# Expert MLP on one core: the last two results in one tile of 8 KB rows, and two weight loads cut differently

## The chip, the core and the metric

One core of a Trainium2 chip runs the kernel. The metric is device time in microseconds (us). Each number of the kernel before is from three runs, or from one further execution taken with the hardware profiler. The engines are named as in the profile: PE multiplies, PEld loads weights for it, DVE, ACT and POOL are the vector, scalar and general engines, and SP only issues transfers. SP, ACT and POOL each have a queue (SPq, ACTq, POOLq) in which instructions wait in order. All transfers are carried by the core's 16 DMA engines; the profile calls POOL's transfer queue q0, SP's q1, ACT's q10, and q8 and q14 carry instructions.

## The reference

Eight experts, each with 256 tokens (`capacity`), a hidden size of 512 and an inner size of 2048, all float32:

```
h   = maximum(x @ w1 + b1, 0)     # [8, 256, 2048]
out = h @ w2 + b2                 # [8, 256, 512]
```

The inputs `w1` and `w2` are 4 MB per expert each. The output is 512 KB per expert, 4 MB in all.

## The kernel before, in words

The names: `E` is 8 experts, `T` 256 tokens, `H` 512, `M` 2048, `P` 128 partitions, `nTB` = 2 token blocks, `nKC` = 4 slices of H, `nJ` = 16 slices of M. All weights are read by POOL's transfers, which cast float32 to float16 on the way: 2 MB land in SBUF for each 4 MB read. `w1_pool` and `w2_pool` hold three experts each.

The loop at the end of the function has E + LAG steps (`LAG` = 3). Step `s` makes the first product of expert `s` and the second product of expert `s - 3`. The first product (`first_product`) makes `hT` in 16 slices, each of four matmuls into `ph` and one ACT activation with the bias. The second product (`second_product`) starts two PSUM tiles `po0` and `po1`, one for each token block, with a one-row matmul that adds b2, and then adds 16 matmuls to each. It goes through `w2` in the same pieces in which `w2` was loaded: for a whole tile, first all 16 matmuls of `po0` and then all 16 of `po1`; for a tile in halves, 8 matmuls of `po0` and 8 of `po1` with the first half, and then the same with the second. PE's matmuls keep the order of the program (`ordered`), and so do POOL's transfers.

The order of the loads is written into a list, `ring`: at step `s` those entries are put into POOL's queue whose step has come. The loads of `w2` stand there in the order of the experts, and behind the last of them stand the two stores that `flush` makes, 2 MB for experts 0 to 3 and 1 MB for experts 4 and 5.

Results are gathered in `store`. `GROUPS` says which experts share a tile: 0 to 3 with rows of 16 KB, 4 and 5 with rows of 8 KB. In a group of n experts the token order is such that each expert fills P/n partitions with rows of n * nTB * H values. ACT's activation writes `hT` in the matching order (`split`), and DVE copies `po0` in n pieces and ACT `po1` in n pieces. Experts 6 and 7 are in no group: each has a tile of its own from `out_pool`, with rows of 4 KB, one DVE copy and one ACT copy. Expert 6 is stored in three parts, 25 rows by SP, 96 by ACT and 7 by SP (`PARTS`), and expert 7 by SP in one transfer of 128 rows, which is the last thing that the kernel starts. `HALVED` names the experts whose `w2` is loaded and used in halves: 6 and 7.

Of the kernel before, what the change touches and what calls it, by code (L numbers as in the profile page):

```python
# [10 lines left out]
def kernel(  # L11
# [9 lines left out]
    nc = tc.nc  # L21
    fp32 = mybir.dt.float32
    fp16 = mybir.dt.float16
    E, T, H = x.shape
    M = w1.shape[2]
    P = 128
    nTB = T // P
    nKC = H // P
    nJ = M // P
    B = 32  # L30
    nB = P // B
    LAG = 3

    GROUPS = {0: 4, 4: 2}
    HALVED = (E - 2, E - 1)


    PARTS = {E - 2: ((0, 25, False), (25, 121, True), (121, 128, False))}  # L40
    nXF32 = 2
    X_LOADS = {2: 2, 4: 4}

    def ordered(ins):
        return tc.keep_in_program_order(ins)
# [7 lines left out]
    group_pool = ctx.enter_context(tc.tile_pool(name="groups", bufs=1))  # L53
    out_pool = ctx.enter_context(tc.tile_pool(name="outp", bufs=2))
# [11 lines left out]
    w2_sb = [None] * E  # L66
    hT = [None] * E
    pending = {}
    results = {}
    group_of = {first + i: (first, n) for first, n in GROUPS.items() for i in range(n)}  # L70

    def load_x(first, n):

        R = n * T // P
        t = x_pool.tile([P, R, H], fp16, tag=f"x{first}", name=f"x{first}")
        ordered(nc.gpsimd.dma_start(  # L76
            out=t, in_=x[first : first + n].rearrange("e (p r) h -> (e p) r h", r=R)
        ))
        for i in range(n):
            x16[first + i] = (t, i * (P // n), R)  # L80
# [7 lines left out]
    def load_w2(e):  # L88
        src = w2[e].rearrange("(p j) h -> p j h", j=nJ)
        w2_sb[e] = w2_pool.tile([P, nJ, H], fp16, tag="w2", name="w2sb")  # L90
        half = nJ // 2 if e in HALVED else nJ
        for lo in range(0, nJ, half):
            ordered(nc.gpsimd.dma_start(out=w2_sb[e][:, lo : lo + half], in_=src[:, lo : lo + half]))  # L93

    def transposes(e):


        t, p0, R = x16[e]
        n = R // nTB
        xT[e] = xT_pool.tile([P, nKC, T], fp16, tag="xT", name="xT")  # L100
        for g in range(T // R // B):
            src = t[p0 + B * g : p0 + B * (g + 1)]
            for b in range(nB):
                block = src[:, :, b * (H // nB) : (b + 1) * (H // nB)].rearrange(
                    "p (n tb) (i kc) -> p tb kc n i", tb=nTB, kc=nKC)
                out = xT[e][b * B : (b + 1) * B].rearrange(
                    "p kc (tb g i n) -> p tb g kc n i", tb=nTB, i=B, n=n)
                if n == 1:
                    nc.vector.transpose(out=out[:, :, g, :, 0, :], in_=block[:, :, :, 0, :])  # L109
                    continue  # L110
                for tb in range(nTB):
                    nc.vector.transpose(out=out[:, tb, g], in_=block[:, tb])  # L112

    def first_product(e):
        hT[e] = hT_pool.tile([P, nJ, T], fp16, tag="hT", name="hT")
        split = group_of[e][1] if e in group_of else 1
        for j in range(nJ):
            bias_at = j * B + e * nB + nB - 1
            ph = psum_h.tile([P, T], fp32, tag="ph", name="ph")
            for kc in range(nKC):  # L120
                ordered(nc.tensor.matmul(  # L121
                    out=ph,
                    lhsT=w1_sb[e][:, kc, :].rearrange("p (q j) -> p q j", j=nJ)[:, :, j],
                    rhs=xT[e][:, kc, :],
                    start=(kc == 0),
                    stop=(kc == nKC - 1),
                ))
            nc.scalar.activation(  # L128
                out=hT[e][:, j, :].rearrange("p (tb k i) -> p tb k i", tb=nTB, k=split),
                in_=ph.rearrange("p (tb i k) -> p tb k i", tb=nTB, k=split),  # L130
                func=mybir.ActivationFunctionType.Relu,
                bias=b1T[:, bias_at : bias_at + 1],
                scale=1.0,
            )
            if j == nJ // 2 and e + 1 < E:
                transposes(e + 1)
# [3 lines left out]
        ordered(nc.gpsimd.dma_start(out=dst, in_=src))  # L140

    def store(e, po):
        if e in group_of:
            first, n = group_of[e]
            split, rows = n, P // n
            if e == first:
                results[e] = group_pool.tile(
                    [P, split * nTB, H], fp32, tag=f"out{e}", name=f"out{e}")
        else:
            first, n, split, rows = e, 1, 1, P  # L150
            results[e] = out_pool.tile([P, nTB, H], fp32, tag="out", name="out")
        out_sb = results[first]
        at = (e - first) * rows
        for k in range(split):
            part = slice(k * rows, (k + 1) * rows)
            nc.vector.tensor_copy(out=out_sb[at : at + rows, k * nTB, :], in_=po[0][part])  # L156
            nc.scalar.copy(out=out_sb[at : at + rows, k * nTB + 1, :], in_=po[1][part])  # L157
        dst = out[first : first + n].rearrange("e (p r) h -> (e p) r h", r=split * nTB)
        if e in group_of:
            if e == first + n - 1:  # L160
                pending[first] = (dst, out_sb)
            return
        for p0, p1, scalar in PARTS.get(e, ((0, P, False),)):
            (nc.scalar if scalar else nc.sync).dma_start(out=dst[p0:p1], in_=out_sb[p0:p1])

    def second_product(e):
        po = []
        for tb in range(nTB):
            t = psum_o.tile([P, H], fp32, tag=f"po{tb}", name=f"po{tb}")
            po.append(t)  # L170
            ordered(nc.tensor.matmul(  # L171
                out=t, lhsT=ones1, rhs=b2_sb[0:1, e * H : (e + 1) * H], start=True, stop=False,
            ))
        half = nJ // 2 if e in HALVED else nJ
        for lo in range(0, nJ, half):
            for tb in range(nTB):
                for j in range(lo, lo + half):
                    ordered(nc.tensor.matmul(  # L178
                        out=po[tb],
                        lhsT=hT[e][:, j, tb * P : (tb + 1) * P],  # L180
                        rhs=w2_sb[e][:, j, :],
                        start=False,
                        stop=(j == nJ - 1),
                    ))
        store(e, po)

    x32 = []
    for e in range(nXF32):
# [4 lines left out]
        out=b2_sb,  # L193
        in_=b2.rearrange("e h -> (e h)").rearrange("(o f) -> o f", o=1),
# [12 lines left out]
    for b in range(nB):  # L207
        nc.vector.transpose(  # L208
            out=b1T[b * B : (b + 1) * B, nB - 1 - b : nB - 1 - b + nJ * B],
            in_=b1_rows.rearrange("r (i j) -> r j i", j=nJ),  # L210
# [4 lines left out]
    ring = []  # L215
    for s in range(1, E + LAG - 1):
        if s < E:
            if s in X_LOADS:
                ring.append((s - 2, load_x, (s, X_LOADS[s])))
            ring.append((s - 2, load_w1, (s,)))  # L220
        if s >= LAG:
            ring.append((s - 2, load_w2, (s - LAG,)))
    ring.append((E + LAG - 3, load_w2, (E - 1,)))
    for first, n in GROUPS.items():
        ring.append((first + n + LAG, flush, (first,)))

    for s in range(E + LAG):
        while ring and ring[0][0] <= s:
            _, put, args = ring.pop(0)
            put(*args)  # L230
        if s < E:
            first_product(s)
        if s >= LAG:
            second_product(s - LAG)
# [31 lines left out]
```

## Time and profile before

| | us |
|---|---|
| median of 3 runs (lowest to highest) | 181.59 (181.48 to 181.77) |
| the profiled execution, own time | 181.45 |
| its span in the trace | 179.7 |
| PE busy in the span | 129.1 |
| DVE busy | 88.0 |
| ACT busy | 70.2 |
| last matmul ends | 173.31 |
| last store issued by SP | 173.9 |

The span begins with the first instruction and ends with the last one. Sums on the trace are made in the span's time; the profiled execution took 1.75 us more than its span, and lies 0.14 us under the median. Besides instructions the trace holds one record for each DMA packet, with its queue, size, start and duration, but without the engine that carried it. A packet here is one row of a transfer: 16 KB, 8 KB or 4 KB as it is written.

### The profile page before, as it was taken

Reading aid. Unit: us, or ns where it says so; the run is one execution under the profiler, and the core shown is the slowest. Engines: PE = TensorE matmul, PEld = TensorE weight load, DVE = VectorE, ACT = ScalarE, POOL = GpSimd, SP = SyncE. Lnnn points to the kernel's source line nnn. Section 1 sums busy time; section 2 is a strip of 40 time slices with the busy share of each in tenths; the row PEclk is TensorE's granted clock in tenths of the full one; section 3 lists DMA queues with packets and bytes.
Section 4 is the critical chain, followed back from the end, with each engine's and each line's share of the span. In section 5 each row is a group of like instructions: output and inputs, shape, how many; then the busy total and the mean of one; then the engine's idle time right before and its main releaser. Section 6 shows DMA issues by size and latency. Waiting matters only on the chain.

```text
span 179.7 us, 1958 instructions
## 1 busy us (share of the span) xinstructions
PE 129.1 (72%) x784; PEld 85.8 (48%) x784; DVE 88.0 (49%) x125; ACT 70.2 (39%) x151; POOL 13.1 (7%) x28
## 2 busy tenths in 40 slices
PE   0005099969595970899969597969497887999950
PEld 0004079969592320795369244844195332433420
DVE  0999942987000199999999998003200020301010
ACT  0000459969593022483099005950586020020010
POOL 7000002120201010001010001000200021010000
PEclk9999999999998798589999889999999996999996
DMA  5999999999999999999999999999999999999996
GB/s 216 251 226 199 233 212 197 233 224 193 228 230 192 221 233 215 197 230 230 204 208 230 219 193 233 226 193 222 230 215 197 233 206 204 223 212 215 335 420 250
DMA packets 3829, 40.56 MB, mean 226 GB/s; under 512 B 461, under 2 KB 477, under 8 KB 1133
## 3 DMA queue, kind: packets, MB, share of 16 engines
q0 software_dynamic: 3232, 38.35, 96.6%
q1 hardware_dynamic: 476, 1.70, 2.4%
q10 hardware_dynamic: 112, 0.39, 0.5%
q8 instruction: 6, 0.10, 0.2%
q14 instruction: 3, 0.02, 0.0%
HBM read 71.39 MB, written 4.19 MB: 421 GB/s over the span
## 4 chain that ended last, share of the span: by engine, by line
DMA 66%; PE 26%; POOL 2%; another core or an unknown queue 1%; issue 1%; ACT 0%; POOLq 0%
DMA w1sb<-in_w_dram 44%; DMA w2sb<-in_w_dram 22%; PE po L178 18%; PE ph L121 8%; PE po L171 1%; POOL w1sb L84 1%; ACT out L157 0%; POOL x L76 0%; POOL b_sb L192 0%; POOL b_rows L196 0%; POOLq L250 0%
## 5 line engine op out<-in xcount | busy, mean ns | idle before, releaser
L121 PE MATMUL ph<-xT,w1sb 128*128 128x256 f16 x512 | 63.6, 289 | 34.8 <-DMA w1sb<-in_w_dram 23.9
L121 PEld LDWEIGHTS <-w1sb 128*128 128x128 f16 x512 | 59.0, 147 | 40.3 <-DMA w1sb<-in_w_dram 32.6
L178 PE MATMUL po<-w2sb,hT 128*128 128x512 f16 x256 | 61.4, 402 | 9.4 <-DMA w2sb<-in_w_dram 9.4
L112 DVE STREAM_TRANSPOSE xT<-x 32x256 f16<-32x256 f16 (+1 forms) x64 | 53.1, 889 | 25.6 <-DMA x<-in_x_dram 18.7
L128 ACT ACTIVATE hT<-ph,b1T 128x256 f16<-128x256 f32 x128 | 56.2, 474 | 13.6 <-PE ph L121 13.4
L178 PEld LDWEIGHTS <-hT 128*128 128x128 f16 x256 | 25.9, 102 | 44.7 <-issue 19.3
L156 DVE COPY out<-po 32x512 f32<-32x512 f32 (+2 forms) x22 | 15.1, 688 | 54.0 <-PE po L178 53.8
L157 ACT COPY out<-po 32x512 f32<-32x512 f32 (+2 forms) x22 | 12.7, 579 | 69.7 <-PE po L178 69.5
L109 DVE STREAM_TRANSPOSE xT<-x 32x256 f16<-32x256 f16 x32 | 14.0, 436 | 0.5
L93 POOL DMA_DIRECT2D w2sb<-in_w_dram x10 | 5.3, 534 | 72.8 <-PE po L178 72.8
L128 ACT ACT_TABLE_LOAD x1 | 1.3, 1283 | 20.5 <-DVE b1T L208 20.5
L84 POOL DMA_DIRECT2D w1sb<-in_w_dram x8 | 4.5, 558 | 63.2 <-PE ph L121 62.4
L171 PE MATMUL po<-b_sb,ones 1*128 1x512 f16 x16 | 4.8, 379 | 0.0
L208 DVE STREAM_TRANSPOSE b1T<-b_rows 32x512 f32<-32x512 f32 x4 | 4.1, 1035 | 0.1
L201 DVE CAST x<-x 128x1024 f16<-128x1024 f32 x2 | 1.5, 757 | 3.3 <-DMA x<-in_x_dram 3.3
L140 POOL DMA_DIRECT2D out_dram<-out x2 | 1.1, 542 | 10.9 <-ACT out L157 10.9
L171 PEld LDWEIGHTS <-ones 1*128 1x128 f16 x16 | 0.9, 92 | 2.1 <-issue 2.1
L76 POOL DMA_DIRECT2D x<-in_x_dram x2 | 1.1, 552 | 0.0
L197 DVE MEMSET ones<- 1x128 f16 x1 | 0.2, 165 | 0.8 <-PEq L250 0.8
L196 POOL DMA_DIRECT2D b_rows<-in_b_dram x1 | 0.5, 515 | 0.0
L192 POOL DMA_DIRECT2D b_sb<-in_b_dram x1 | 0.5, 513 | 0.0
L250 POOL MEMSET const-float32-0.0<- 128x1 f32 x1 | 0.1, 99 | 0.2 <-issue 0.2
(3 smaller groups left out, 0.3 us busy)
## 6 DMA issues: line engine op xcount, KB each, us to landing
w1sb<-in_w_dram POOLq DMA_DIRECT2D x8, 2048.0 KB, 34.5
w2sb<-in_w_dram POOLq DMA_DIRECT2D x6, 2048.0 KB, 46.8
w2sb<-in_w_dram POOLq DMA_DIRECT2D x4, 1024.0 KB, 24.0
out_dram<-out POOLq DMA_DIRECT2D x1, 2048.0 KB, 26.8
x<-in_x_dram SPq DMA_DIRECT2D x2, 512.0 KB, 3.9
x<-in_x_dram POOLq DMA_DIRECT2D x1, 1024.0 KB, 30.8
out_dram<-out POOLq DMA_DIRECT2D x1, 1024.0 KB, 17.8
x<-in_x_dram POOLq DMA_DIRECT2D x1, 512.0 KB, 24.0
```

The lines of the kernel that those rows point to most:

```text
L84: ordered(nc.gpsimd.dma_start(out=w1_sb[e], in_=w1[e].rearrange("(p kc) m -> p kc m", kc=nKC)))
L93: ordered(nc.gpsimd.dma_start(out=w2_sb[e][:, lo : lo + half], in_=src[:, lo : lo + half]))
L109: nc.vector.transpose(out=out[:, :, g, :, 0, :], in_=block[:, :, :, 0, :])
L112: nc.vector.transpose(out=out[:, tb, g], in_=block[:, tb])
L121: ordered(nc.tensor.matmul(out=ph, lhsT=w1_sb[e][:, kc, :].rearrange("p (q j) -> p q j", j=nJ)[:, :, j], rhs=xT[e][:, kc, :], start=(kc == 0),
L128: nc.scalar.activation(out=hT[e][:, j, :].rearrange("p (tb k i) -> p tb k i", tb=nTB, k=split), in_=ph.rearrange("p (tb i k) -> p tb k i", ...
L156: nc.vector.tensor_copy(out=out_sb[at : at + rows, k * nTB, :], in_=po[0][part])
L157: nc.scalar.copy(out=out_sb[at : at + rows, k * nTB + 1, :], in_=po[1][part])
L171: ordered(nc.tensor.matmul(out=t, lhsT=ones1, rhs=b2_sb[0:1, e * H : (e + 1) * H], start=True, stop=False,))
L178: ordered(nc.tensor.matmul(out=po[tb], lhsT=hT[e][:, j, tb * P : (tb + 1) * P], rhs=w2_sb[e][:, j, :], start=False, stop=(j == nJ - 1),))
L201: nc.vector.tensor_copy(out=t, in_=x32[e])
L208: nc.vector.transpose(out=b1T[b * B : (b + 1) * B, nB - 1 - b : nB - 1 - b + nJ * B], in_=b1_rows.rearrange("r (i j) -> r j i", j=nJ),)
```

## The change

Experts 6 and 7 become a third group, with one tile of 8 KB rows: partitions 0 to 63 belong to expert 6, 64 to 127 to expert 7. Their copies are therefore of 64 partitions, two on DVE and two on ACT for each expert. The tile is stored in four parts, rows 0 to 4, 5 to 9, 10 to 15 and 16 to 127, all by SP and in this order. SP waits twice: before the first part for expert 6's copies, since the first three parts hold results of expert 6 alone, and before the last part for expert 7's copies. ACT issues no store any more.

The weights `w2` of expert 5 are loaded and used in two halves instead of whole, those of expert 7 in pieces of 8, 4 and 4 slices instead of 8 and 8.

```diff
-    GROUPS = {0: 4, 4: 2}
-    HALVED = (E - 2, E - 1)
-    PARTS = {E - 2: ((0, 25, False), (25, 121, True), (121, 128, False))}
+    GROUPS = {0: 4, 4: 2, 6: 2}
+    PIECES = {E - 3: (8, 8), E - 2: (8, 8), E - 1: (8, 4, 4)}
+    PARTS = ((0, 5), (5, 10), (10, 16), (16, P))
...
+    def pieces(e):
+        at, spans = 0, []
+        for n in PIECES.get(e, (nJ,)):
+            spans.append((at, at + n))
+            at += n
+        return spans
...
-        half = nJ // 2 if e in HALVED else nJ
-        for lo in range(0, nJ, half):
-            ordered(nc.gpsimd.dma_start(out=w2_sb[e][:, lo : lo + half], in_=src[:, lo : lo + half]))
+        for lo, hi in pieces(e):
+            ordered(nc.gpsimd.dma_start(out=w2_sb[e][:, lo:hi], in_=src[:, lo:hi]))
...
-        for k in range(split):
-            part = slice(k * rows, (k + 1) * rows)
-            nc.vector.tensor_copy(out=out_sb[at : at + rows, k * nTB, :], in_=po[0][part])
-            nc.scalar.copy(out=out_sb[at : at + rows, k * nTB + 1, :], in_=po[1][part])
+        for tb in range(nTB):
+            for k in range(n):
+                to = out_sb[at : at + rows, k * nTB + tb, :]
+                part = po[tb][k * rows : (k + 1) * rows]
+                if tb == 0:
+                    nc.vector.tensor_copy(out=to, in_=part)
+                else:
+                    nc.scalar.copy(out=to, in_=part)
...
-        for p0, p1, scalar in PARTS.get(e, ((0, P, False),)):
-            (nc.scalar if scalar else nc.sync).dma_start(out=dst[p0:p1], in_=out_sb[p0:p1])
+        for p0, p1 in PARTS:
+            ordered(nc.sync.dma_start(out=dst[p0:p1], in_=out_sb[p0:p1]))
...
-        half = nJ // 2 if e in HALVED else nJ
-        for lo in range(0, nJ, half):
+        for lo, hi in pieces(e):
             for tb in range(nTB):
-                for j in range(lo, lo + half):
+                for j in range(lo, hi):
...
     for first, n in GROUPS.items():
-        ring.append((first + n + LAG, flush, (first,)))
+        if first + n < E:
+            ring.append((first + n + LAG, flush, (first,)))
```

The order of instructions on PE, DVE and POOL is otherwise that of before; POOL issues two more loads.

More of the change, by code (lines that the diff above doesn't have):

```diff
@@ L115, in first_product @@
         hT[e] = hT_pool.tile([P, nJ, T], fp16, tag="hT", name="hT")
-        split = group_of[e][1] if e in group_of else 1
+        split = group_of[e][1]
         for j in range(nJ):
@@ L142, in store @@
     def store(e, po):
[L143 to L151, printed above, removed]
+        first, n = group_of[e]
+        rows = P // n
+        if e == first:
+            results[e] = group_pool.tile([P, n * nTB, H], fp32, tag=f"out{e}", name=f"out{e}")
         out_sb = results[first]
         at = (e - first) * rows
-        for k in range(split):
-            part = slice(k * rows, (k + 1) * rows)
-            nc.vector.tensor_copy(out=out_sb[at : at + rows, k * nTB, :], in_=po[0][part])
[L157 to L161, printed above, removed]
-            return
-        for p0, p1, scalar in PARTS.get(e, ((0, P, False),)):
-            (nc.scalar if scalar else nc.sync).dma_start(out=dst[p0:p1], in_=out_sb[p0:p1])
+        for tb in range(nTB):
[6 more added lines that the diff above has]
+                    nc.scalar.copy(out=to, in_=part)
+        if e < first + n - 1:
+            return
+        dst = out[first : first + n].rearrange("e (p r) h -> (e p) r h", r=n * nTB)
+        if e < E - 1:
+            pending[first] = (dst, out_sb)
+            return
+        for p0, p1 in PARTS:
+            ordered(nc.sync.dma_start(out=dst[p0:p1], in_=out_sb[p0:p1]))
     def second_product(e):
```

## The prediction
> **What bounds the kernel now.** I read the page's slices first, then the chain of waits, the stretches of the tail, the queues, and last the records of single DMA packets.
>
> ```profile
> span 179.7 us, 1958 instructions
> ...
> DMA  5999999999999999999999999999999999999996
> ...
> HBM read 71.39 MB, written 4.19 MB: 421 GB/s over the span
> ...
> q0 software_dynamic: 3232, 38.35, 96.6%
> q1 hardware_dynamic: 476, 1.70, 2.4%
> q10 hardware_dynamic: 112, 0.39, 0.5%
> q8 instruction: 6, 0.10, 0.2%
> ```
>
> The DMA engines are full in every slice but the first and the last: 75.6 MB at 421 GB/s is the span. So time can only come from bytes, from the cost of a packet, from engines that end at different times, or from the 1.25 us between the last packet and the end. The chain of waits tells another story:
>
> ```profile
> 110.12 39.38 DMA w2sb<-in_w_dram
> 149.50 0.04 issue
> 149.54 8.66 PE po L178 x32
> 158.20 0.53 PE po L171 x2
> 158.74 7.01 PE po L178 x32
> 165.75 0.53 PE po L171 x2
> 166.28 7.03 PE po L178 x32
> 173.31 0.02 issue
> 173.33 0.59 ACT out L157
> ```
>
> It says that PE runs 24 us without a break once w2 of expert 5 has landed whole, and that this sets the last store. The stretches of the tail say what that is worth:
>
> ```profile
> 149.50:153.00 3.50, 3.46 (x9) 1.23 (x9) 0.00 (x0) 0.00 (x0) 0.00 (x0) 0.53 1.04 218
> ...
> 173.30:175.30 2.00, 0.00 (x0) 0.00 (x0) 0.00 (x0) 0.59 (x1) 0.00 (x0) 1.00 0.99 412
> 175.30:177.00 1.70, 0.00 (x0) 0.00 (x0) 0.00 (x0) 0.00 (x0) 0.00 (x0) 0.91 0.96 405
> 177.00:178.40 1.40, 0.00 (x0) 0.00 (x0) 0.00 (x0) 0.00 (x0) 0.00 (x0) 0.50 0.68 275
> 178.40:179.70 1.30, 0.00 (x0) 0.00 (x0) 0.00 (x0) 0.00 (x0) 0.00 (x0) 0.50 0.00 0
> ```
>
> (The last three columns are PE's clock, DMA share, GB/s.) DMA is still full four us after PE's last matmul: the stores of experts 0 to 5, 3 MB, lie in q0 behind the last load. It thins out only at 177 to 178.4, where engines finish one after another.
>
> The packet records show which. Chained by their ends, they give 16 sequences. Each has work to the end, with no gap in the tail, and its part of the last store (q1, 8 packets) begins the moment its q0 is empty, first at 175.79. The sequences fall into three kinds. Five (call them A) carry 25 of the rows of expert 6 that SP stores early, five each, and one more of the 7 rows; they end at 178.07 to 178.42. Six (B) each carried one of the 16 KB instruction packets of q8, 0.93 us; two of them also have one of the 7 rows; they end at 178.13 to 178.43. The other five (C) end at 177.05 to 177.55. So the early rows fill A up to about what the instruction packets cost B, and the end is the last of eleven nearly even engines, 178.43; the span's end is 1.25 us behind it.
>
> **The change part by part.**
>
> *PE's chain.* Step of a 16 KB packet of a cast load is 1.21 us, of an 8 KB one 0.606 us. Half of expert 5's w2 is thus there 4.85 us before 149.50, at 144.7, while PE is busy with expert 4 until 146.85. Expert 5 then runs from 147.4 (0.6 us for the two bias matmuls) without a wait: 32 matmuls at 0.22 us (7.05 us by the two later products), to 154.5. Its 2.09 us wait and the slow clock behind it (8.66 against 7.05) go. Next the landings bound PE. The slowest engine's last packets of expert 6's halves end at 154.06 and 158.9, its first half of expert 7 at 163.8 and the last piece at 168.9; PE sees them 0.33 us later (149.17 in the records, 149.50 in the chain). Expert 6: 155.1 to 158.6, wait to 159.25, to 162.8. Expert 7: bias, wait to 164.2, eight slices to 167.7, four to 169.45, the last four from 169.45 to 171.2. ACT now has two copies of 64 partitions behind it, 2 x 0.58 instead of one of 0.59, and SP issues at 172.4 instead of 173.9. The gain of 1.5 us at this point is hidden whole: no engine of A or B has room for the store before its other work is done. DVE's two copies (0.69 us each) end before ACT's.
>
> *Is the larger last store still in time?* It has 112 rows of 8 KB, seven per engine at a step of 0.305 us (the stores of experts 4 and 5 have rows of this size): 2.14 us where there were 8 x 0.155 = 1.24. The last engines run dry without it at 178.5 - 2.14 = 176.35. From issue to first packet took 1.9 us at most before (173.91 to 175.79), so an issue up to 174.4 costs nothing. That leaves 2.0 us.
>
> *Added packets.* Whole, expert 5's w2 took 9.69 us on one engine from first packet to the next transfer's first (138.31 to 148.00), expert 6's in halves 9.73 us (148.00 to 157.73). A cut costs 0.04 us per engine, its semaphore packet included. Expert 5 gets one cut, expert 7 one more. 4 KB cast packets took 0.324 us against 0.625 for 8 KB, the same excess per cut, so 0.04 each: +0.08 on every engine.
>
> The Trainium skill, "DMA: Bandwidth & Descriptors", section "Anatomy of one DMA — SWDGE (gpsimd) path", speaks against such cuts: each transfer has about 2.0 us fixed beside its bytes. Taken as time on the path, two more loads would by that page be an estimated +4 us. The 0.04 us here is the measured price where transfers stand in a queue, and the sum goes by it.
>
> *Stores of 6 and 7.* On B before, 6 + 8 packets of 4 KB at 0.155: 2.17 us; now 7 x 0.305 = 2.135: -0.035. On A six more before, 20 x 0.155 = 3.10; now 7 + 3 = 10 x 0.305 = 3.05: -0.05. This takes it that 5, 5 and 6 rows begin on the same engines, as the 7 rows did with those of the 25; the sixth row of the third part then falls on one engine of B, which has one of the 7 rows now: from 2.325 to 2.44, +0.115. The records of the 25 and 7 show this placing, so I take it over an even spread.
>
> *Waits and queues.* SP's three small parts wait for expert 6's copies, about 164, and the last part behind them for expert 7's; only these stand in SP's queue, 0.36 us each. ACT loses a 0.38 us issue, which hid nothing. POOL issues two more loads (0.53 us each) at 110 and 147, with 17 us of waiting for PE before each; the store of experts 0 to 3 behind the latter goes 0.53 us later into a queue 20 us deep: nothing. ACT's strided read for experts 6 and 7: 0.474 us per activation at 130.9 with group size 2 and in all others alike, nothing. The 2 MB store waits for nothing new.
>
> *Sum.* A: +0.08 - 0.05 = +0.03, to 178.45. B: +0.08 - 0.035, to 178.475. The one engine of B: its 178.13 or 178.27 + 0.195, at most 178.46. The end moves by +0.05 us: 179.75 span, 181.50 own time. The execution lies 0.14 under the median, so 181.64.
>
> Unknown on both sides: in each sequence one or two of the last load packets before the stores took 0.03 to 0.4 us longer, on 14 or so of the 16, unevenly (sequences without it exist in A and B). Their cause is not in the trace. Gone on all, A and B would gain 0.15 to 0.4, but the engine with the sixth row has none to lose: gain at most 0.1 on the end. Twice as large on one engine of B: +0.25. The range keeps both.
>
> **Rivals.**
>
> *The last store too late (slower).* PE now waits three times, twice for about 0.8 us. A wait of 2.09 us at 149.5 was followed by a clock of 0.53 and a product 1.6 us longer; one of 1.94 at 139.85 by full clock. If experts 6 and 7 both fell into it, SP would issue at 175.6, 1.2 us beyond 174.4: 182.85. It decides from an issue at 174.4 on. For: more waits. Against: they are shorter than those that did nothing.
>
> The skill's "TensorE: Matmul & The Clock Gate", section "HAM oscillation — how this bites in real kernels", wants idle gaps over about 3.4 us for a slow clock; the 2.09 us wait here contradicts it, and by either the issue comes before 174.4 unless it happens twice.
>
> *The rows fall elsewhere (slower).* If the 16 early rows go one to each engine, B gains 0.305 to 178.78 (+0.35); if three lie on an engine of B, +0.9: 182.0 to 182.55. Against: the placing of the 7 rows.
>
> *Less disturbance (faster).* ACT's store of 96 rows was issued at 166.40, in the time in which the last load packets were slow; if such issues slow them and all go, the end gains 0.1 by the sum, 0.4 if the sixth row lies in C: 181.2. Against: one of the slow packets (165.47) started and ended before 166.40, and others at 167.4 followed undisturbed ones.
>
> *It doesn't do what it says* would be PE still bound by its own order; then SP issues at 173.9, still before 174.4: same time.
>
> **How the numbers follow.** About 0.2%, 0.36 us, is what a measurement of this kernel can tell from no change. My case, the end set by full DMA engines with a shift of -0.1 to +0.3: 0.62 (within 0.2% nearly always). Late store 0.10, rows elsewhere 0.16, half of that just above 0.36, less disturbance 0.12, more than half of it beyond 0.2%. Faster 0.12, same 0.60, slower 0.28. Range: from 181.2 (less disturbance) to 182.3, inside the slower cases; the likeliest case alone 181.5 to 181.9.
>
> **What would show it.** Right: last matmul near 171, SP's last issue near 172.4, last packet at 178.3 to 178.7, DMA full to 177, first q1 packets of the last store between q0's. Each step: expert 5's product about 7.05 us from 147.4; 9.73 us for its w2; the early rows on A. Wrong: a gap between q0's end and the last store on some engine, an engine ending past 178.8, or all ending before 178.1.

## The result: 0.5% slower, and the profile after

The changed kernel took 182.61 us (median of 6 runs, 182.06 to 182.98) against 181.59 (181.48 to 181.79): a ratio of 1.0053, interval 1.0032 to 1.0074. I had forecast no change, 181.64, range 181.2 to 182.3.

The profiled execution is the slowest of its six, 182.98 us with a span of 181.2; a second profile below (d_changed) took 182.42 with a span of 180.6, near the median. From the page and its queues:

```profile
span 181.2 us, 1961 instructions
...
DMA  6998998999899999998999999999999999999992
...
HBM read 71.39 MB, written 4.19 MB: 417 GB/s over the span
...
q0 software_dynamic: 3520, 38.35, 95.8%
q1 hardware_dynamic: 448, 2.10, 3.1%
q8 instruction: 6, 0.10, 0.2%
```

The bytes are the same and the engines are as full; the rate over the span fell by 1%. The last digit shows where: DMA is busy there for a fifth of the slice instead of six tenths. PE did what it was meant to do (timeline: start, duration, instruction, wait before it):

```profile
147.39 7.08 PE L183 MATMUL po<-w2sb,hT 128*128 128x512 f16 x32
...
159.32 3.61 PE L183 MATMUL po<-w2sb,hT 128*128 128x512 f16 x16 [0.76 <-DMA w2sb<-in_w_dram]
...
164.17 8.78 SPq L170 DMA_DIRECT2D out_dram<-out  x4
164.20 7.20 PE L183 MATMUL po<-w2sb,hT 128*128 128x512 f16 x32 [0.73 <-DMA w2sb<-in_w_dram]
...
171.44 1.17 ACT L162 COPY out<-po 64x512 f32<-64x512 f32 x2 [7.29 <-PE po L183]
```

Expert 5 starts at 147.39, two waits of 0.7 us follow, PE is done at 171.4 instead of 173.3, and SP issues the last store at 172.63 instead of 173.94. The time was lost after all of that. The stretches of the tail, to be set beside those of before:

```profile
175.30:177.00 1.70, 0.00 (x0) 0.00 (x0) 0.00 (x0) 0.00 (x0) 0.00 (x0) 0.78 0.98 390
177.00:178.40 1.40, 0.00 (x0) 0.00 (x0) 0.00 (x0) 0.00 (x0) 0.00 (x0) 0.50 0.58 240
178.40:179.70 1.30, 0.00 (x0) 0.00 (x0) 0.00 (x0) 0.00 (x0) 0.00 (x0) 0.50 0.07 32
```

In the last row 0.07 is one engine of sixteen, busy alone. DMA was as busy as before from 175.3 to 177 (0.98 against 0.96), but moved less (390 against 405 GB/s): some packets take longer for the same bytes. The DMA view of 176 to 181, in 40 slices, shows the lone engine as single rows of 8 KB. The kernel before, in the same window, has nothing behind 178.43:

```profile
DMA  8969999499873877531000000000000000000000
```

The changed kernel:

```profile
DMA  9989499497946667130101001010010000000000
GB/s 655 328 262 590 197 524 393 197 524 262 393 197 262 262 262 328 66 131 0 66 0 66 0 0 66 0 66 0 0 66 0 0 0 0 0 0 0 0 0 0
```

The packet records name it. On that engine the last five rows of the 1 MB store (q0) start at 174.91 and take 0.605, 0.614, 0.635, 0.447 and 0.594 us, where 0.309 is usual. Only then come its seven rows of the last store, at the usual pace, from 177.83 to 179.98. The other fifteen engines end much as before: five between 177.08 and 177.34 (before: five between 177.04 and 177.55) and ten between 177.96 and 178.56 (before: eleven between 178.07 and 178.43). The last packet lies 1.55 us later than before (179.98 against 178.43), and this execution took 1.53 us more than the profiled one before (182.98 against 181.45), so the one engine accounts for the time. In the time of the five slow rows, a few of the other engines' rows of the last store are slow too (0.33 to 0.72).

### The profile page after: what moved, and what is told of

Same layout as the page of the kernel before. It is cut to its first block, busy times and chain, and to the rows that moved or that the text cites. A ratio compares the mean times of both kernels' runs of the same rounds, so it can differ in the third digit from the quotient of the medians.

```text
span 181.2 us, 1961 instructions
## 1 busy us (share of the span) xinstructions
PE 127.7 (70%) x784; PEld 85.4 (47%) x784; DVE 89.3 (49%) x127; ACT 71.2 (39%) x153; POOL 14.1 (8%) x30
## 4 chain that ended last, share of the span: by engine, by line
DMA 53%; PE 33%; ACT 3%; another core or an unknown queue 2%; POOL 2%; issue 1%; ACTq 0%; POOLq 0%
DMA w1sb<-in_w_dram 44%; PE po L183 18%; PE ph L127 14%; DMA w2sb<-in_w_dram 9%; ACT out L162 3%; PE po L177 1%; POOL w1sb L91 1%; ACT hT L134 1%; ACTq L267 0%; POOL b_sb L197 0%; POOL x L83 0%; POOL b_rows L201 0%; POOLq L256 0%
## 5 line engine op out<-in xcount | busy, mean ns | idle before, releaser
L183 PE MATMUL po<-w2sb,hT 128*128 128x512 f16 x256 | 60.2, 395 | 8.0 <-DMA w2sb<-in_w_dram 8.0
L160 DVE COPY out<-po 32x512 f32<-32x512 f32 (+1 forms) x24 | 16.5, 688 | 52.4 <-PE po L183 52.1
L162 ACT COPY out<-po 32x512 f32<-32x512 f32 (+1 forms) x24 | 13.9, 578 | 66.6 <-PE po L183 66.5
L99 POOL DMA_DIRECT2D w2sb<-in_w_dram x12 | 6.4, 536 | 70.9 <-PE po L183 70.9
```

The lines of the kernel that those rows point to most:

```text
L99: ordered(nc.gpsimd.dma_start(out=w2_sb[e][:, lo:hi], in_=src[:, lo:hi]))
L160: nc.vector.tensor_copy(out=to, in_=part)
L162: nc.scalar.copy(out=to, in_=part)
L183: ordered(nc.tensor.matmul(out=po[tb], lhsT=hT[e][:, j, tb * P : (tb + 1) * P], rhs=w2_sb[e][:, j, :], start=False, stop=(j == nJ - 1),))
```

## The experiments

Three theories were formed on this. *Crossing*: the last store is dealt to the engines as seven rows each, and these, so the theory, lie in other partitions than the rows that each engine has in a store of 128 rows; where two engines then draw on the same place, both or one of them wait. *Early issue*: the last store comes sooner and overlaps the 1 MB store. *Wide rows*: two stores with rows of 8 KB side by side disturb each other. Four kernels on one chip (before: 181.69):

**a_loads**, the kernel before with only the loads cut:

```diff
-    HALVED = (E - 2, E - 1)
+    PIECES = {E - 3: (8, 8), E - 2: (8, 8), E - 1: (8, 4, 4)}
```

> The kernel before with only the loads cut as in the change (w2 of expert 5 in halves, of expert 7 in 8, 4, 4); stores as before, from tiles of 4 KB rows. Crossing theory (the last store of 112 rows, seven per engine, gets in the way of one engine's part of the 1 MB store): no such store here, so only the two cuts count, +0.05 to +0.15 us on 181.6, PE's last matmul at about 171, no store packet of double length. Early-issue theory (the last store now arrives while the 1 MB store still runs, because PE ends 2 us earlier): as in the changed kernel, 182.0 to 183.0, with packets of double length on one engine. Wide-row theory (two stores with rows of 8 KB side by side): as crossing.

Measured: 182.0, ratio 1.003 (1.0013 to 1.0048). There is no packet of double length among the stores, so the disturbance isn't made by the early issue alone; but the loss is larger than the +0.08 us that I had given the cuts. The last packet ends at 178.65 (+0.22 against before). The rest, 0.3 us, lies behind it and is taken up under f_pool_last.

**b_stores**, the changed kernel with the loads of before:

```diff
-    PIECES = {E - 3: (8, 8), E - 2: (8, 8), E - 1: (8, 4, 4)}
+    PIECES = {E - 2: (8, 8), E - 1: (8, 8)}
```

> The changed kernel with the loads of before (w2 of expert 5 whole, of expert 7 in halves), so only the stores are changed. Crossing theory and wide-row theory: the loss stays, 182.0 to 183.0, one engine with packets of the 1 MB store at 0.6 us instead of 0.31 and an end a microsecond behind the others. Early-issue theory: the last store is issued at about 174.5 as before, so no loss, 181.5 to 181.8.

Measured: 181.9, ratio 1.0018 (1.0004 to 1.0033). The stretched packets are there, 36 of them with 4.1 us too much in all, but spread over many engines and almost all in the last store itself; of the 1 MB store only one row is longer (0.375). Last packet at 178.94. So the place of the disturbance was right and its form was not: no single engine is left behind.

**c_one_store**, the changed kernel with one last store:

```diff
-    PARTS = ((0, 5), (5, 10), (10, 16), (16, P))
+    PARTS = ((0, P),)
```

> The changed kernel with all 128 rows of the last tile in one store at the end instead of 5, 5, 6 and 112. Nothing fills the engines that had no instruction packet, so the six others end last, one row of 0.305 us more than with seven: about 181.9 to 182.0 in all. Crossing theory: eight rows per engine are placed as those of the other stores are, no packet is doubled, 181.9 to 182.0. Wide-row and early-issue theories: packets of double length are still there and the time is 182.4 or more.

Measured: 182.01, ratio 1.0015 (1.0004 to 1.0026), not one stretched packet. The ends are those of an uneven load, 177.50 to 178.00 on ten engines and 178.52 to 179.05 on six. DMA view, 176 to 181:

```profile
DMA  7999979999796633633314000000000000000000
GB/s 328 393 459 459 459 328 459 459 459 393 328 524 262 262 131 131 262 131 131 131 66 197 0 0 0 0 0 0 0 0 0 0 0 0 0 0 0 0 0 0
```

The rows are as wide and the issue as early (172.76) as in the changed kernel. Wide rows and early issue alone are out as the cause of the stretched packets.

**d_changed**, the changed kernel again.

> The changed kernel once more, for a second profile. If the loss has a fixed place (crossing theory), again one engine has several 8 KB packets of the 1 MB store at about 0.6 us and ends 0.5 to 1.5 us behind the other fifteen; if it is chance, another kind of packet is slow, or none.

Measured: 182.42, ratio 1.0051 (1.0036 to 1.0065). Again one engine ends last, at 179.42, 0.62 behind the next, and three rows of the 1 MB store are stretched (0.515, 0.522, 0.952) beside eleven of the last store. Two of the three (0.515 and 0.952, 0.85 too much) lie on the engine that ends last. The last packet is 0.99 us later than in the profile before, and the execution 0.97 longer (182.42 against 181.45). On the same chip, then, taking the balancing parts away (c) made the kernel better by 0.36% of the time before, although it makes the load of the engines less even by 0.3 us.

Next, on another chip (before: 181.77), whether seven rows per engine do it with narrow rows too, what partitions have to do with it, and what a_loads lost.

**g_narrow112**, the kernel before with its last store in two:

```diff
-    PARTS = {E - 2: ((0, 25, False), (25, 121, True), (121, 128, False))}
+    PARTS = {E - 2: ((0, 25, False), (25, 121, True), (121, 128, False)),
+             E - 1: ((16, P, False), (0, 16, False))}
```

> The kernel before with the last store, 128 rows of 4 KB, in two: rows 16 to 127 and then rows 0 to 15. Each engine still gets eight rows, seven and one. Crossing theory: 112 rows are dealt to the engines seven in a row, which are other partitions than those that the engine has in the 1 MB store, so packets are stretched in the tail as in b_stores: 181.8 to 182.4. Wide-row theory (8 KB rows beside 8 KB rows): no stretched packets, 181.6 to 181.7.

Measured: 182.44, ratio 1.0036 (1.0017 to 1.0055). Rows of 4 KB, loads as before, each engine's share as before, and still six rows of the 1 MB store take 0.34 to 0.84 us and rows of the last store up to 0.49 instead of 0.159; the last packet ends at 179.24. One row of the 1 MB store (0.84) ends at 177.96, and eight rows of 0.159 lead from there to that end. DMA view of 176 to 181, with single rows at the end as in the changed kernel:

```profile
DMA  9969499595993658854520000000000000000000
GB/s 492 426 262 623 197 492 426 197 393 197 361 426 131 262 229 361 328 229 164 230 98 0 33 33 33 0 0 0 0 0 0 0 0 0 0 0 0 0 0 0
```

That is as the crossing theory had it, with nothing else of the change. The run also adds a store of 16 rows, whose issue took SP until 176.06. Engines without other work got its row only near 178.1, but they end by 178.43 and don't set the end.

**h_half64**, b_stores with the 112 rows in two parts:

```diff
-    PARTS = ((0, 5), (5, 10), (10, 16), (16, P))
+    PARTS = ((0, 5), (5, 10), (10, 16), (16, 64), (64, P))
```

> b_stores (stores of the change, loads of before) with the 112 rows in two parts, rows 16 to 63 with the early ones and rows 64 to 127 last. Less is left for the end, 0.5 MB. If stretched packets come from partitions (the engines draw from a few partitions' worth of the same port when rows lie in one half of the tile): the last store's packets are at about 0.6 us on all engines, 182.0 to 183.0. If they come from where the rows are written: the last store's packets at 0.31 us, few stretched, 181.5 to 181.8, about the kernel before.

Measured: 183.47, ratio 1.0091 (1.0057 to 1.0125), the slowest of all, with 10.8 us too much in 45 packets. This is neither of the two outcomes expected: of 75 rows of the last two parts behind 175.3, 25 took 0.33 us or more, most often 0.63, and the others 0.31. Three rows of the 2 MB store were stretched too (0.764, 0.792 and 1.365 instead of 0.61). The Trainium skill, "SBUF — State Buffer", section "Door 1: The DMA port swizzle (why `[64,N]` ≈ `[32,N]`)", says that 64 partitions of one half reach only half of the ports. The rows at twice the length would fit two engines on one port; the many normal ones don't follow from it. No run here shows which partition an engine reads, so whether the place in common is a port of SBUF or a place in the output's memory stays open.

**f_pool_last**, the kernel before with the last store behind POOL's others:

```diff
+        if e == E - 1:
+            last.append((dst, out_sb))
+            return
...
+    dst, src = last.pop()
+    ordered(nc.gpsimd.dma_start(out=dst, in_=src))
```

> The kernel before with the last store issued by POOL behind its other two instead of by SP, same rows. The amount of work on the DMA engines is the same. Late-drain theory: all ends on q0 at about 178.4, POOL's drain ends 1.4 us later, at 179.85 instead of SP's 178.92, so +0.9 us: 182.4 to 182.6. If the drain is not what counts: 181.5 to 181.8.

Measured: 182.61, ratio 1.0036 (1.0013 to 1.006); the profiled execution took 182.41. The last packet ends at 178.48, as before (178.43), and yet the span is 0.9 us longer. The DRAIN instructions of the kernel's closing line say why; first before, then f_pool_last (shortest, median and longest in ns, first and last start):

```profile
L261 POOLq DRAIN  x3: 45/93/18881, 159.7 to 179.4; - x3
L261 SPq DRAIN  x3: 7/7/7, 178.9 to 179.2; - x3
```

```profile
L266 POOLq DRAIN  x3: 45/92/5947, 173.9 to 180.3; - x3
L266 SPq DRAIN  x3: 7/7/7, 178.9 to 180.1; - x3
```

POOL's long drain ends at 159.7 + 18.88 = 178.57 before, 1.4 us behind q0's last packet (177.19), ahead of SP at 178.9, 0.5 us behind q1's last packet. In f_pool_last it ends at 173.9 + 5.95 = 179.87, again 1.4 us behind q0, and everything waits for it. SP is ready at 178.9 here too, 0.5 us behind the last packet, though that packet is q0's and SP's own queue had ended at 174.78: in this run SP's wait follows the last store packet of any queue. In a_loads:

```profile
L266 POOLq DRAIN  x3: 45/97/23465, 156.0 to 179.9; - x3
L266 SPq DRAIN  x3: 7/7/7, 179.1 to 179.7; - x3
```

The last store, issued at 172.81, takes turns with the 1 MB store on some engines, q0's last packet moves to 177.99, POOL's drain ends at 179.44, and SP, ready at 179.1, waits 0.3 us. This is the part of a_loads's loss that the packets don't explain, in that execution.

**e_halves5** (`HALVED = (E - 3, E - 2, E - 1)`) and **j_cut7** (`PIECES = {E - 2: (8, 8), E - 1: (8, 4, 4)}`), the two cuts singly, the second on a third chip (before: 181.71), as are all runs below.

> The kernel before with w2 of expert 5 in halves and nothing else changed. The loads of the change cost 0.3% in a_loads, more than the 0.08 us of added packets. Late-drain theory (the cuts end PE sooner, the last store comes sooner and takes turns with the 1 MB store, POOL's queue q0 empties later, and POOL's last drain needs 1.4 us from there where SP needs 0.5): with expert 7 still in halves PE ends only 0.4 us sooner, so hardly anything of that: 181.6 to 181.8, q0's last packet before 177.5. Cut-cost theory (each cut costs some 0.15 us by itself): 181.8 to 181.9, with q0's last packet where it was.

> The kernel before with w2 of expert 7 in 8, 4 and 4 and expert 5 whole. PE is still bound by its own order from 149.5 on and issues the last store at about 173.9 as before. Late-drain theory: only the added packets, 181.6 to 181.75. Cut-cost theory: half of a_loads's loss, 181.8 or more.

Measured: 181.95, ratio 1.0009 (0.999 to 1.0029), and 181.91, ratio 0.9999 (0.9982 to 1.0015). Neither is clear of no change, and both intervals take in 0.15 us (0.08%), so they neither show nor rule out a price of that size for each cut. In the profile of e_halves5 one engine got through its loads a microsecond later than the others of its kind, and the last packet ended at 179.36; why was not followed up. In that of j_cut7 PE was not held up as expected: its product of expert 5 ran at full clock (7.07 us from 149.57), SP issued at 172.38, and POOL's drain ended 0.15 behind SP.

**k_loads_again**, a_loads a second time, and **i_loads_sp4**, a_loads with the 1 MB store by SP:

```diff
-        ordered(nc.gpsimd.dma_start(out=dst, in_=src))
+        ordered((nc.sync if first == 4 else nc.gpsimd).dma_start(out=dst, in_=src))
```

> a_loads once more, beside its two neighbours on the same chip. Both theories: 181.9 to 182.1. Late-drain theory: again q0's last packet after 177.7 and POOL's drain ending behind SP's wait for the last store.

> a_loads with the 1 MB store of experts 4 and 5 issued by SP instead of POOL, so that q0 ends with the 2 MB store. It now takes turns with the loads of w2, which land about 2.5 us later, so PE ends near 173.6 and SP issues the last store near 175. Late-drain theory: q0's last packet before 177, POOL's drain no longer the last, so a_loads's loss of 0.3 us at the end is gone: 181.6 to 181.8 unless engines run dry before the last store, which the trace would show as gaps. Cut-cost theory: as a_loads, 182.0 or more.

Measured: 182.05, ratio 1.0013 (1.0000 to 1.0027), and 182.15, ratio 1.0017 (1.0000 to 1.0035). In k_loads_again q0 ended at 178.02, but SP and POOL were ready together (179.43, 179.46), so here the drain cost nothing; the last packet itself ended at 178.96, 0.52 later than before. In i_loads_sp4 POOL's drain ended first (179.05, SP at 179.36), and the time did not come back: the loads, now sharing the engines with 1 MB of stores, made PE later still (last issue at 175.82), and the last packet ended at 178.89. The run is no test of the drain.

**l_aligned**, b_stores with `PARTS = ((0, P),)`.

> b_stores with the whole tile of experts 6 and 7 in one store of 128 rows of 8 KB (loads of before). Crossing theory: eight rows per engine from the partitions that the engine has in the 1 MB store too, so no stretched packet; the ends by balance 0.3 us later than before on six engines, 0.6 earlier on five: 181.7 to 182.0. Wide-row theory: packets stretched as in b_stores, 182.0 or more.

Measured: 182.03, ratio 1.001 (0.9994 to 1.0026). No packet is doubled; 25 rows of the last store take 0.33 instead of 0.31, 0.45 us too much in all, where b_stores had 4.1. With the loads of before, too, a last store of rows 16 to 127 makes long packets, and one of all 128 rows does not. The runs don't part the row count from the first row. Nor is another row count than 128 enough by itself: in the kernel before, ACT's store of 96 rows of expert 6 (from row 25 on) ran beside the 2 MB store, and 35 of its rows started after the 1 MB store's first row at 173.18; all 96 took the usual 0.159 us.

No kernel here is faster than the kernel before.

## Why the prediction was wrong, step by step

*Bound.* Right: full DMA engines set the end, and PE's 2 us were worth nothing. *PE's chain.* Right to 0.3 us: last matmul 171.4 (171.2), issue 172.63 (172.4), expert 5 in 7.08 from 147.39.

*Added packets and placing of the early rows.* Fifteen engines ended by 178.56, where the sum had 178.48, and five of them ended early, as before; so the two cuts, the 8 KB rows and the early rows on five engines came out near their prices together. Each price by itself is not shown. The slow last packets of the loads, which I had left open, nearly vanished (four packets with 0.02 to 0.10 too much), without a gain at the end. And with the loads alone the last packet came 0.22 and 0.52 us later (a_loads, k_loads_again), where the sum had +0.08.

*Is the larger last store still in time, and the stores of 6 and 7.* This is the step that failed. "Seven per engine at a step of 0.305 us" took the price of a row from the 1 MB store, whose 128 rows lie with the engines in one way, for a store of 112 rows. That these lie with the engines in another way is the theory; that they took longer is measured. In the profile above, single rows of the last store took up to 0.72 us, and five rows of the 1 MB store 0.58 on average. On one engine that is 2.895 - 5 x 0.309 = 1.35 us, nearly the whole of the 1.42 between 178.56 and 179.98. The same step gave the earlier issue as free: "an issue up to 174.4 costs nothing". With 112 rows this is not shown: in b_stores, issued at 174.65, one row of the 1 MB store was stretched, by 0.07, and in the two profiles of the changed kernel, both issued at 172.63, five and three. But in g_narrow112, issued at 173.88, it was six, so the early issue is not needed for it. Nor does the loss go by the sum of the long packets: b_stores, with the loads of before, had 4.1 us too much, spread over many engines, and lost 0.18%; the changed kernel had about 2 us in the profile above, 1.35 of them on one engine, and lost 0.5%.

*The 1.25 us behind the last packet* I had taken as fixed. It is the later of two ends, POOL's drain 1.4 us behind q0 and SP's wait 0.5 behind the last store packet. In the changed kernel SP's was later by 1.2, so this term wasn't the cause there:

```profile
L267 POOLq DRAIN  x3: 45/93/23335, 155.9 to 180.9; - x3
L267 SPq DRAIN  x3: 7/7/7, 180.4 to 180.7; - x3
```

POOL's long drain ends there at 179.28. In a_loads the term was 0.3 us, in k_loads_again nothing. That the ratios of a_loads and b_stores add up to that of the change is therefore no proof of two independent losses.

*Rivals.* None of them was the cause. "The rows fall elsewhere" had the right sign and an end past 178.8 on one engine, but by bytes, which stayed even. "The last store too late" had the wrong direction, since it came early. It counts three waits of PE, where the working of PE's chain has two; the trace shows two from expert 5 on (0.76 and 0.73 us), both followed by full pace.

What stays open: why the packets of these stores stretch and those of the 96 rows did not, what two engines have in common when it happens, what decides which engine gets the long packets, and how the loads' share (0.13 to 0.30% in two tries) divides into added packets and POOL's drain.

## What to carry to other kernels

In this kernel DMA is full nearly to the end, and the end is the slowest of sixteen engines; equal bytes per engine were not equal time. Before a store is cut to even out the load, look in the packet records whether its rows keep their packet time while another store runs. Rows 16 to 127 cost more than the 0.3 us of imbalance that they were to remove: one store of all 128 was better by 0.36%. And a transfer that is issued earlier on one queue can end another queue later (q0 at 177.99 instead of 177.19 in a_loads), so ask which queue's end the kernel's last instructions wait for, and how long each takes from there: with the same last packet, the last store cost 0.9 us more in the span when POOL issued it.

## What the runs showed that I had not expected

A store of rows 16 to 127 stretched packets of a store on another queue, to twice their time and more (0.605 to 0.635 us with rows of 8 KB, up to 0.84 with rows of 4 KB, against 0.309); stores of 128 rows did not. POOL's drain ends 1.4 us behind its queue's last packet (177.19 to 178.57, 177.99 to 179.44, 178.48 to 179.87), SP's wait 0.5 us behind the last store packet (178.43 to 178.92, and 178.48 to 178.99 where POOL's queue had it).
